# A decoder step in fp32: embedding first, S5 matrices on VectorE, products in column groups, last units by halves

## The chip, the cores and the metric

The kernel runs on one core of a Trainium2 chip. The metric is the device time of one execution in microseconds (us); a comparison uses the median over runs. The engines are named as in the profile: PE is TensorE (matmuls; PEld its weight loads), DVE is VectorE, ACT is ScalarE, POOL is GpSimd, and SP is SyncE, which here only issues DMAs.

## The reference

One inference step of a two-layer recurrent trunk, in fp32, for 512 prompt tokens and 8x8 sample tokens that share the weights. `h` is the stream of 1024 features by 576 tokens:

```python
for i in range(DEPTH):
    hn = rmsnorm(h, norm_mix[i])
    out = ab_mixer(hn) if i % 2 == 0 else cd_mixer(hn)
    h = h + out
    hn = rmsnorm(h, norm_ff[i])
    h = h + square(relu(hn @ w_ff1[i])) @ w_ff2[i]
    gate = sigmoid(rmsnorm(h, norm_ple[i]) @ w_ple_gate[i])
    h = h + gate * (p[i] @ w_ple_proj[i])
y = rmsnorm(h, norm_final)
```

`ab_mixer` holds an mLSTM and a retention (four heads each), `cd_mixer` an HGRN2 and an S5 state-space model with 32 groups of 16 channels and 64 complex states each. `rmsnorm(x, g)` is x / sqrt(mean(x^2) + 1e-6) * g over the 1024 features. The new states are outputs as well.

## The kernel before

The stream `h` lies in eight tiles of 128 features x 576 tokens. Every large product runs as three fp32r matmuls: an operand is split into a rounded high part and the rest, and hi*hi, hi*lo and lo*hi are added. A **unit** (`unit`, L222 to L232) is one 128x1024 block of weights: a DMA on SP's queue brings `wr`, ACT casts it to `wh` (L229), DVE subtracts to `wl` (L230), and `cols` runs 48 matmuls of 128x288 tokens (`mm3`, L238: 8 slices of the contraction, 3 products, 2 halves of the tokens). Inputs are split the same way: `xh` on ACT (L273) and `xl` on DVE (L274), for the MLP's middle `uh` (L270) and `ul` (L271).

`norm` makes the split inputs and the sum of squares `sqa`; its `stat` reduces the sum over partitions by a matmul with ones (L331), takes Ln and Exp(-0.5 x) on ACT and one Newton step on DVE, L279 to L281. `load` brings the embedding `pin` of layer 0, the first weights and `h`, multiplies the embedding (`po`, L361) and stores the eight results to DRAM from POOL's queue (L362); `po` has three buffers. `embed_in` loads and splits `pin`.

The S5 model turns into ordinary products with matrices that are made on the chip during the first MLP. `s5_tables` and `s5_turn` compute complex powers with many small DVE operations (128x32 and larger). `elem(ct)`, L1093 to L1109, builds a quarter of two matrices, ET and G: two multiplications and a sum for each, 128x1024 and 128x1152, with operands that are broadcast. `prod(ct, q)`, L1111 to L1137, transposes four groups of ET (L1120) and multiplies each with G into the rows 0 to 15 of a PSUM bank (L1121); ACT copies both out, and DMAs write them to DRAM. These pieces are hooks between the units of `ff` (layer 0): `elem` before a block, `prod` at its sixth and eighth unit.

`ple(1)` runs the last eight units. Six are ordinary: z = product * r (L481), tanh (L482), two DVE operations into `h` (L483, L484). `finish` does the last two by halves of the tokens, 288 each: for both halves the units, squares and the final statistic (L398, L399), Ln, Exp and Newton, and behind both the eight scalings of each half (L412) with a store each on SP's queue (L413).

The Tile framework orders the instructions: it places them by priority (`high_priority`, `issue_after`) and keeps each engine's stream in one order. An engine that waits holds back everything behind it in its stream.

Of the kernel before, what the change touches and what calls it, by code (L numbers as in the profile page):

```python
# [9 lines left out]
F32 = mybir.dt.float32  # L10
# [160 lines left out]
class K:  # L171
# [61 lines left out]
    def mm3(self, ps, wh, wl, xh, xl, first, last, halves=(0, 1)):  # L233

        mm = self.nc.tensor.matmul
        for a, b in ((wh, xh), (wh, xl), (wl, xh)):
            for j in halves:
                mm(ps[:, j, :HALF], a, b[:, j * HALF:(j + 1) * HALF],  # L238
                   start=first and a is wh and b is xh, stop=last and a is wl)
# [42 lines left out]

    def rsqrt(self, r, m, t):
# [9 lines left out]
    def norm(self, g, first=None, dve=False, tables=True):  # L293
# [17 lines left out]
        def stat():  # L311
            if not done:
                done.append(1)
                with self.tc.high_priority(400):
                    make()
            return r

        def make():

            tt = nc.vector.tensor_tensor  # L320
            hi, lo = (self.np_.tile([P, NT], F32R, name=f"sq{i}", tag="sq") for i in "hl")
            tt(acc[0], acc[0], acc[1], ALU.add)
# [10 lines left out]
            m, q = acc  # L333
            for j in range(2):
                s = slice(j * HALF, (j + 1) * HALF)
                nc.scalar.activation(r[:, s], ps[j], AF.Ln, bias=self.eps, scale=1.0 / D)
                nc.vector.tensor_scalar(m[:, s], ps[j], 1.0 / D, EPS, ALU.mult, ALU.add)
            nc.scalar.activation(r, r, AF.Exp, scale=-0.5)
            self.stat_done = self.newton(r, m, q)
# [26 lines left out]
    def embed_in(self, l, pool, eng, xp=None):  # L366
        self.xple = []
        for k in range(2):
            t = pool.tile([P, NT], F32, name="pin", tag="fu")
            eng.dma_start(t, self.A["pT"][l, k])  # L370
            self.xple.append(self.split(t, pool=xp or pool))

    def finish(self, n0, gate, pt):
# [14 lines left out]
        ws, rs = [gate(n) for n in range(n0, KD)], []  # L388
        for j in range(2):
            s = slice(j * HALF, (j + 1) * HALF)  # L390
            pst = self.pmt()[:, :HALF]
            for n, one in zip(range(n0, KD), ws):
                last = one(j)
# [7 lines left out]
            m, q, r = (pt.tile([P, HALF], F32, name=f"f{i}", tag=f"f{i}") for i in range(3))  # L401
            with self.tc.issue_after(last.ins):
                nc.scalar.preload_act_table_set("natural_log_exp_and_others")
            nc.scalar.activation(r, pst, AF.Ln, bias=self.eps, scale=1.0 / D)
            nc.vector.tensor_scalar(m, pst, 1.0 / D, EPS, ALU.mult, ALU.add)
            nc.scalar.activation(r, r, AF.Exp, scale=-0.5)
            self.newton(r, m, q)
            rs.append(r)
        for j in range(2):
            s = slice(j * HALF, (j + 1) * HALF)  # L410
# [1146 lines left out]
```

## Time and profile before

| | |
|---|---|
| median of 3 runs | 1700.53 us (1698.25 to 1702.41) |
| the profiled execution | 1699.72 us |
| its span in the trace | 1697.9 us |
| busy: PE / DVE / ACT / POOL | 1622.4 / 1004.9 / 604.4 / 308.0 us |
| granted PE clock, mean | 0.984 |
| moved by DMA | 168.92 MB |
| chain that ended last | PE 82%, DVE 10%, ACT 3%, DMA 3% |

The span is the time from the first to the last event of the profiled execution; 1.8 us lie around it. Times inside the trace count from the span's start. A row of a timeline gives start, duration, engine, line, operation, out<-in, shapes, count, and in brackets the idle time ahead of it and who ended it. Consecutive matmuls overlap in the pipeline, so the distance of two starts, not the duration, is the cost of one. The granted clock is the share of 2.4 GHz.

### The profile page before, as it was taken

How to read it: one execution, taken by the hardware profiler on the slowest of the kernel's cores; microseconds unless marked ns; L12 is line 12 of the kernel's file. 1: busy time of each engine (PE TensorE's matmuls, PEld its weight loads, DVE VectorE, ACT ScalarE, POOL GpSimd, SP SyncE). 2: the span in 40 equal slices, each digit the busy share in tenths (PEclk: the TensorE clock that was granted, in tenths of full speed). 3: DMA queues.
4: the chain of work that ended last, by engine and by line, in shares of the span. 5: the costliest groups of instructions: out<-in, count | busy, mean ns of one | idle time of the engine just before them, and what ended most of it. 6: DMA issues, size and time to landing. Idle time of an engine off the chain costs nothing.

```text
span 1697.9 us, 28934 instructions
## 1 busy us (share of the span) xinstructions
PE 1622.4 (96%) x11973; PEld 1564.9 (92%) x11973; DVE 1004.9 (59%) x1796; ACT 604.4 (36%) x952; POOL 308.0 (18%) x256
## 2 busy tenths in 40 slices
PE   6999999999899999999999789989999999999996
PEld 5999799999799999999999788979999999999996
DVE  5878665668943634447576797386643333334456
ACT  5333222235213223133443344362531323314354
POOL 1321232211300302003022565232100000000100
PEclk9999999999899999999999899999999999999998
DMA  6322222223222323324427322522222222222222
GB/s 247 108 80 89 99 82 89 78 78 114 92 92 93 123 87 95 114 87 142 143 71 222 119 72 68 151 84 64 75 86 77 88 87 78 85 88 92 85 87 69
DMA packets 77219, 168.92 MB, mean 99 GB/s; under 512 B 29088, under 2 KB 34080, under 8 KB 76960
## 3 DMA queue, kind: packets, MB, share of 16 engines
q1 hardware_dynamic: 76008, 164.20, 29.8%
q8 instruction: 94, 1.54, 0.4%
q0 software_dynamic: 640, 2.36, 0.3%
q10 hardware_dynamic: 440, 0.52, 0.1%
q14 instruction: 37, 0.30, 0.1%
HBM read 142.91 MB, written 24.13 MB: 98 GB/s over the span
## 4 chain that ended last, share of the span: by engine, by line
PE 82%; DVE 10%; ACT 3%; DMA 3%; issue 2%; SPq 0%; POOL 0%; ACTq 0%; DVEq 0%; POOLq 0%
PE pb L238 73%; PE pm L737 1%; PE pm L507 1%; DVE wl L230 1%; DVE e L1356 1%; DVE e L1358 1%; PE pm L1367 1%; PE pm L757 1%; PE pm L1121 1%; DMA s5U<-yd 1%; ACT xh L273 1%; PE pm L774 0%; DMA prd<-po 0%; DVE s5w L1204 0%; PE pm L849 0%
## 5 line engine op out<-in xcount | busy, mean ns | idle before, releaser
L238 PE MATMUL pb<-xh,wh 128*128 128x288 f32 x2480 | 544.0, 300 | 31.0 <-ACT wh L229 12.4
L238 PE MATMUL pb<-xl,wh 128*128 128x288 f32 x2480 | 542.7, 298 | 1.0 <-DVE xl L274 1.0
L238 PE MATMUL pb<-xh,wl 128*128 128x288 f32 x2480 | 543.1, 298 | 0.0
L229 ACT CAST wh<-wr 128x1024 fp32r<-128x1024 f32 x219 | 229.7, 1049 | 757.4 <-PE pb L238 701.5
L238 PEld LDWEIGHTS pb<-xh,wh 128*128 128x128 f32 x2480 | 402.7, 190 | 41.7 <-ACT wh L229 14.7
L238 PEld LDWEIGHTS pb<-xl,wh 128*128 128x128 f32 x2480 | 403.8, 190 | 6.1 <-issue 4.2
L238 PEld LDWEIGHTS pb<-xh,wl 128*128 128x128 f32 x2480 | 403.2, 190 | 3.6 <-issue 2.9
L230 DVE TENSOR_TENSOR wl<-wr,wh 128x1024 fp32r<-128x1024 f32 x199 | 251.0, 1261 | 22.8 <-ACT wh L229 13.5
L238 PE MATMUL pb<-ul,wh 128*128 128x288 f32 x1024 | 220.0, 296 | 6.6 <-DVE ul L271 6.6
L238 PE MATMUL pb<-uh,wl 128*128 128x288 f32 x1024 | 219.9, 296 | 1.5 <-DVE wl L230 1.5
L238 PE MATMUL pb<-uh,wh 128*128 128x288 f32 x1024 | 219.6, 296 | 0.2 <-ACT uh L270 0.2
L441 DVE TENSOR_TENSOR h<-h,pb 128x576 f32<-128x576 f32 x64 | 48.2, 753 | 214.0 <-PE pb L238 214.0
L238 PEld LDWEIGHTS pb<-ul,wh 128*128 128x128 f32 x1024 | 165.1, 189 | 6.8 <-DVE ul L271 6.8
L238 PEld LDWEIGHTS pb<-uh,wl 128*128 128x128 f32 x1024 | 165.0, 189 | 1.7 <-DVE wl L230 1.7
L238 PEld LDWEIGHTS pb<-uh,wh 128*128 128x128 f32 x1024 | 164.7, 189 | 0.8 <-issue 0.4
L428 DVE SCALAR_TENSOR_TENSOR fu<-pb,r 128x576 f32<-128x576 f32 x64 | 48.5, 757 | 185.5 <-PE pb L238 185.5
L308 POOL TENSOR_TENSOR sqa<-sqa,sq 128x576 f32<-128x576 f32 x20 | 32.8, 1640 | 502.1 <-ACT sq L307 481.3
L230 POOL TENSOR_TENSOR wl<-wr,wh 128x1024 fp32r<-128x1024 f32 x20 | 50.6, 2534 | 82.2 <-ACT wh L229 77.4
L271 DVE TENSOR_TENSOR ul<-fu,uh 128x576 fp32r<-128x576 f32 x64 | 52.3, 819 | 9.6 <-ACT uh L270 9.2
L1105 POOL TENSOR_TENSOR s5ET<-s5bc,s5y 128x1024 f32<-128x1024 f32 x4 | 8.3, 2066 | 260.7 <-PE pm L1121 221.2
L735 POOL TENSOR_TENSOR Vm<-V,cc 64x384 f32<-64x384 f32 (+3 forms) x36 | 34.6, 972 | 106.0 <-ACT V L719 66.8
L429 ACT ACTIVATE fu<-fu 128x576 f32<-128x576 f32 x64 | 43.8, 685 | 10.6 <-DVE fu L428 10.0
(456 smaller groups left out, 1631.7 us busy)
## 6 DMA issues: line engine op xcount, KB each, us to landing
wr<-in_w_dram SPq DMA_DIRECT2D x219, 512.0 KB, 3.5
sR<-Rd SPq DMA_DIRECT2D x12, 256.0 KB, 3.6
h<-in_hT_dram SPq DMA_DIRECT2D x8, 288.0 KB, 6.8
prd<-po POOLq DMA_DIRECT2D x8, 288.0 KB, 4.5
Gd<-s5G SPq DMA_DIRECT2D x4, 576.0 KB, 2.9
prj<-prd SPq DMA_DIRECT2D x8, 288.0 KB, 5.2
sG<-Gd SPq DMA_DIRECT2D x8, 288.0 KB, 6.6
out_yT_dram<-h SPq DMA_DIRECT2D x16, 144.0 KB, 1.9
```

Source lines behind the costliest of these rows:

```text
L229: nc.scalar.copy(hi, raw)
L230: (nc.gpsimd if self.lo_pool else nc.vector).tensor_tensor(lo, raw, hi.bitcast(F32), ALU.subtract)
L238: mm(ps[:, j, :HALF], a, b[:, j * HALF:(j + 1) * HALF], start=first and a is wh and b is xh, stop=last and a is wl)
L271: nc.vector.tensor_tensor(lo, src, hi.bitcast(F32), ALU.subtract)
L273: nc.scalar.mul(hi, src, scale)
L308: (nc.vector if i or dve else nc.gpsimd).tensor_tensor(acc[i], acc[i], t, ALU.add)
L428: nc.vector.scalar_tensor_tensor(self.sv(u), self.pv(ps), 0.0, self.sv(r()), ALU.max, ALU.mult)
L429: nc.scalar.activation(u, u, AF.Square)
L441: nc.vector.tensor_tensor(self.sv(self.h[n]), self.sv(self.h[n]), self.pv(ps), ALU.add)
L507: nc.tensor.transpose(dst, src[:n, t0:t0 + tn], self.ident[:n, :n])
L735: nc.gpsimd.tensor_tensor(Vm, V[:NS, 4, :n].unsqueeze(1).to_broadcast([NS, b1 - b0, n]), self.vmask[:, b0:b1].unsqueeze(2).to_broadcast([N ...
L737: nc.tensor.matmul(ps, Kt[:NS, 4], Vm.rearrange("p b n -> p (b n)"), start=True, stop=True)
```

## The change

- `unit` is divided into `fetch` (the DMA) and `parts` (cast and subtraction). `load` asks for the first weights, then the embedding, then the stream; DVE copies one column of the embedding into the first tile of `h`, so that this tile's DMA has to wait for the embedding. The splits of the embedding come behind both of its DMAs.
- `norm` adds epsilon in the sum of squares and runs Newton on the PSUM sum (`newton_sum`) by halves; two operations per norm (L337) go. The first mixer's statistic loses its raised priority.
- `elem` runs on DVE instead of POOL. `prod` does four transposes and then four products, each into its own 32 output rows; ACT copies the four results one by one.
- The last layer runs four ordinary units and the last four by halves of the tokens: half 0 of units 4 to 7, then half 1. Two units share a PSUM bank; the four weights stay in a pool of their own. The scalings and stores of a half stand right behind its statistic; in half 1 every other store goes to ACT's queue.

```diff
+    def fetch(self, *key):
         i = self.units.add(*key)
         raw = self.wp.tile([P, 8 * P], F32, name=f"wr{i}", tag="wr")
+        self.nc.sync.dma_start(raw, self.A["w"][i])
+        return raw
...
+    def newton_sum(self, r, ps, t):
+        nc = self.nc
+        nc.vector.tensor_tensor(t, r, r, ALU.mult)
+        nc.vector.scalar_tensor_tensor(t, t, -0.5 / D, ps, ALU.mult, ALU.mult)
         return nc.vector.scalar_tensor_tensor(r, t, 1.5, r, ALU.add, ALU.mult)
...
-            tt(acc[0], acc[0], acc[1], ALU.add)
+            stt(acc[0], acc[0], EPS * D / P, acc[1], ALU.add, ALU.add)
...
-                nc.vector.tensor_scalar(m[:, s], ps[j], 1.0 / D, EPS, ALU.mult, ALU.add)
...
             with self.tc.high_priority(60):
-                self.embed_in(0, lp, nc.sync)
-                ws = [self.unit("col2", "w_ple_proj", 0, 0, 0)]
+                raw = self.fetch("col2", "w_ple_proj", 0, 0, 0)
+                pin = self.embed_in(0, lp, nc.sync)
+                ws = [self.parts(raw)]
+                nc.vector.tensor_copy(self.h[0][:, 0:1], pin[1][:, 0:1])
             for k in range(KD):
                 nc.sync.dma_start(self.h[k], self.A["hT"][k])
...
-            tt = nc.gpsimd.tensor_tensor
+            tt = nc.vector.tensor_tensor
...
                 nc.tensor.transpose(pe[:, i * P:(i + 1) * P], ET[:, g].rearrange("p d h -> p (d h)"), self.ident)
-                nc.tensor.matmul(pk[:16, i * P:(i + 1) * P], ET[:, g, 0],
+            for i in range(4):
+                g = 4 * q + i
+                nc.tensor.matmul(pk[32 * i:32 * i + 16, :P], ET[:, g, 0],
                                  G[:, g, 0:8].rearrange("p d h -> p (d h)"), start=True, stop=True)
             f = lambda a: a.rearrange("p g n -> p (g n)")
             nc.scalar.copy(f(E), pe)
-            nc.scalar.copy(f(KT), pk[:16])
+            for i in range(4):
+                nc.scalar.copy(KT[:, i], pk[32 * i:32 * i + 16, :P])
...
-            for n in range(8 if l == 0 else 6):
+            for n in range(8 if l == 0 else 4):
...
+            with self.tc.tile_pool(name="wf", bufs=4) as wf:
+                ws = [self.unit("col", "w_ple_gate", l, n * P, 0, pool=wf) for n in range(4, 8)]
+                banks = {}
+                def gate(n, j):
...
+                self.finish(4, gate, pt)
```

In `finish` the loop over the halves now reads (its first part is as before):

```python
        for j in range(2):
...
            for n in range(n0, KD):
                last = gate(n, j)
...
            self.newton_sum(r, pst, q)
            for k in range(KD):
                stt(self.h[k][:, s], self.h[k][:, s], self.v("final", k), r, ALU.mult, ALU.mult)
                (nc.scalar if j and k % 2 else nc.sync).dma_start(self.A["yT"][k][:, s], self.h[k][:, s])
```

What the scheduler made of it, at three places. First DVE before, where `elem(0)` runs on POOL (L925 to L930 and L1018 to L1023 are the complex powers, L428 `fu`, L230 `wl` of unit 51):

```order
L1008 TENSOR_SCALAR s5y_4979<-s5yi 64x256
L927 TENSOR_TENSOR s5yr<-s5yr,s5p_w 128x32
L928 TENSOR_TENSOR s5yi<-s5p_5051,s5p_5052 128x32
L929 TENSOR_TENSOR s5p_w<-s5p_5052,s5p_5051 128x32
L1018 TENSOR_TENSOR s5p_5049<-s5yr 128x32
L930 TENSOR_TENSOR s5yi<-s5yi,s5p_w 128x32
L1019 TENSOR_TENSOR s5p_5050<-s5yi 128x32
L428 SCALAR_TENSOR_TENSOR fu<-pb,r 128x576
L1020 TENSOR_TENSOR s5p_5049<-s5p_5049,s5p_5050 128x32
L230 TENSOR_TENSOR wl_4991<-wr_4988,wh_4990 128x1024
```

and DVE with the change at the same place (L1126 to L1128 are `elem(0)`, L445 `fu`, L234 `wl` of units 51 and 52, L278 `ul`):

```order
L1126 TENSOR_TENSOR s5ET<-s5bc,s5y_4981 128x1024
L949 TENSOR_TENSOR s5yi<-s5p_5054,s5p_5055 128x32
L1127 TENSOR_TENSOR s5t<-s5bc,s5y_4982 128x8x128
L950 TENSOR_TENSOR s5p_w<-s5p_5055,s5p_5054 128x32
L1039 TENSOR_TENSOR s5p_5052<-s5yr 128x32
L445 SCALAR_TENSOR_TENSOR fu<-pb,r 128x576
L234 TENSOR_TENSOR wl<-wr_4991,wh 128x1024
L1128 TENSOR_TENSOR s5ET<-s5ET,s5t 128x1024
L951 TENSOR_TENSOR s5yi<-s5yi,s5p_w 128x32
L1126 TENSOR_TENSOR s5G<-s5bc,s5w_4975 128x1152
L278 TENSOR_TENSOR ul<-fu,uh 128x576
L1127 TENSOR_TENSOR s5t<-s5bc,s5w_4976 128x1152
```

The six operations of `elem(0)` now stand among the splits of the MLP. Second, PE at the third set of products, before:

```order
L238 MATMUL pb<-xh,wl_6904 128x288 x2
L1120 MATMUL pm<-cc,s5ET 128x128
L1121 MATMUL pm<-s5G,s5ET 16x128
L1120 MATMUL pm<-cc,s5ET 128x128
L1121 MATMUL pm<-s5G,s5ET 16x128
L1120 MATMUL pm<-cc,s5ET 128x128
```

and with the change (L1141 the transposes, L1144 the products, L245 bulk matmuls):

```order
L245 MATMUL pb<-ul,wh 128x288 x2
L1141 MATMUL pm<-cc,s5ET 128x128 x4
L1144 MATMUL pm<-s5G,s5ET 16x128
L245 MATMUL pb<-uh,wl 128x288 x2
L245 MATMUL pb<-uh,wh 128x288 x2
L245 MATMUL pb<-ul,wh 128x288 x2
```

The transposes stand together; of the products one follows them, and the other three come 524 bulk matmuls later. Third, DVE in the tail, before (L469 and L471, L472 are a half unit's z and its way into `h`; L405 and L279 to L281 the statistic of half 0; L412 its scalings):

```order
L405 TENSOR_SCALAR f_17197<-pm 128x288
L469 TENSOR_TENSOR z<-pb,r 128x288
L279 TENSOR_TENSOR f_17198<-f_17199 128x288
L280 SCALAR_TENSOR_TENSOR f_17198<-f_17198,f_17197 128x288
L471 SCALAR_TENSOR_TENSOR z<-z,prj_16661 128x288
L281 SCALAR_TENSOR_TENSOR f_17199<-f_17198,f_17199 128x288
L472 TENSOR_TENSOR h_128<-h_128,z 128x288
L412 SCALAR_TENSOR_TENSOR h_121<-h_121,vec,f_17199 128x288
```

and with the change (L429 the last scalings of half 0, L418 sums of squares of half 1, L501 to L504 unit 7's half 1, L293 the Newton step of half 1):

```order
L429 SCALAR_TENSOR_TENSOR h_127<-h_127,vec,f_17183 128x288
L429 SCALAR_TENSOR_TENSOR h_128<-h_128,vec,f_17183 128x288
L418 TENSOR_TENSOR sqa<-sqa,sq 128x288
L501 TENSOR_TENSOR z<-pb,r 128x288
L418 TENSOR_TENSOR sqa<-sqa,sq 128x288
L503 SCALAR_TENSOR_TENSOR z<-z,prj_16691 128x288
L504 TENSOR_TENSOR h_128<-h_128,z 128x288
L293 TENSOR_TENSOR f_17338<-f_17339 128x288
```

Before, the last half unit's z stands ahead of half 0's scalings; with the change it stands behind all eight of them.

## Rows read from the trace of the kernel before

**Rows 1.** The page: busy us (share) x instructions of each engine.

```profile
PE 1622.4 (96%) x11973; PEld 1564.9 (92%) x11973; DVE 1004.9 (59%) x1796; ACT 604.4 (36%) x952; POOL 308.0 (18%) x256
```

**Rows 2.** Timeline of PE at one set of products.

```profile
537.04 0.43 PE L238 MATMUL pb<-xh,wl 128*128 128x288 f32 x2
537.31 0.27 PE L1120 MATMUL pm<-cc,s5ET 128*128 128x128 f32 x1
...
539.26 0.39 PE L1121 MATMUL pm<-s5G,s5ET 128*16 128x128 f32 x2
539.58 0.53 PE L238 MATMUL pb<-xh,wh 128*128 128x288 f32 x2
```

**Rows 3.** Timeline of PE, 442 to 467 us, units 51 and 52.

```profile
442.81 0.43 PE L238 MATMUL pb<-uh,wh 128*128 128x288 f32 x2
...
457.87 0.85 PE L238 MATMUL pb<-ul,wh 128*128 128x288 f32 x2 [6.60 <-DVE ul L271]
...
462.83 0.53 PE L238 MATMUL pb<-uh,wh 128*128 128x288 f32 x2
...
466.92 0.43 PE L238 MATMUL pb<-uh,wh 128*128 128x288 f32 x2
```

**Rows 4.** Windows of PE: us, busy (x), granted clock, DMA share, GB/s.

```profile
458.00:460.00 2.00, 2.00 (x9) 0.50 0.61 241
```

**Rows 5.** Timeline of POOL at elem(0).

```profile
436.08 2.13 POOL L1105 TENSOR_TENSOR s5ET<-s5bc,s5y 128x1024 f32<-128x1024 f32 x1 [39.47 <-DVE s5y L1007]
```

**Rows 6.** Timeline of DVE, 436 to 455 us.

```profile
436.24 2.02 DVE L927 TENSOR_TENSOR s5yr<-s5yr,s5p_w 128x32 f32<-128x32 f32 x1
...
443.69 1.22 DVE L230 TENSOR_TENSOR wl<-wr,wh 128x1024 fp32r<-128x1024 f32 x1
...
446.24 0.19 DVE L927 TENSOR_TENSOR s5yr<-s5yr,s5p_w 128x32 f32<-128x32 f32 x1
...
451.14 3.26 DVE L230 TENSOR_TENSOR wl<-wr,wh 128x1024 fp32r<-128x1024 f32 x1
```

**Rows 7.** Groups of DVE by form: busy us, mean ns, idle before.

```profile
L770 DVE TENSOR_TENSOR hs<-hs,st 128x512 f32<-128x512 f32 x12 | 8.3, 691 | 0.3
```

**Rows 8.** Timeline of PE at two places of the first mixer.

```profile
72.60 0.71 PE L507 MATMUL pm<-cc,oT 128*128 128x128 f32 x5
73.06 0.38 PE L238 MATMUL pb<-xl,wh 128*128 128x288 f32 x1
...
89.36 1.08 PE L757 MATMUL pm<-s_in,qd 128*32 128x129 f32 x16
90.37 0.40 PE L238 MATMUL pb<-xl,wh 128*128 128x288 f32 x1
90.61 0.43 PE L238 MATMUL pb<-xh,wl 128*128 128x288 f32 x2
```

**Rows 9.** Groups of DVE by form, the norms.

```profile
L337 DVE TENSOR_SCALAR sqa<-pm 128x288 f32<-128x288 f32 x12 | 5.2, 458 | 8.3 <-ACT r L336 8.3
```

**Rows 10.** Tile h, first 40 us: ns (least/median/most), first and last start.

```profile
L352 SPq DMA_DIRECT2D h<-in_hT_dram x8: 328/432/705, 2.1 to 8.9; - x8
```

**Rows 11.** DMA issues of the first 45 us: KB each, median us to landing.

```profile
h<-in_hT_dram SPq DMA_DIRECT2D x8, 288.0 KB, 6.8
```

**Rows 12.** Timeline of ACT, the fourth and the seventh po.

```profile
23.99 1.73 ACT L361 ACTIVATE po<-pb 128x576 f32<-128x576 f32 x3
...
30.36 1.36 ACT L361 ACTIVATE po<-pb 128x576 f32<-128x576 f32 x2 [1.46 <-DMA prd<-po]
```

**Rows 13.** Timeline of PE in the start.

```profile
31.77 0.53 PE L331 MATMUL pm<-sqh,ones 128*128 128x288 f32 x2 [3.70 <-ACT po L361]
```

**Rows 14.** Timeline of PE, its last two rows.

```profile
1681.23 0.65 PE L398 MATMUL pm<-sqa,ones 128*128 128x288 f32 x2
1686.23 1.33 PE L399 MATMUL pm<-sq,ones 128*128 128x288 f32 x2 [4.35 <-ACT sq L395]
```

**Rows 15.** Timeline of DVE, the scalings of the last half.

```profile
1690.88 3.52 DVE L412 SCALAR_TENSOR_TENSOR h<-h,vec,f 128x288 f32<-128x288 f32 x8
```

**Rows 16.** Timeline of ACT in the tail, a table load.

```profile
1675.03 1.28 ACT L403 ACT_TABLE_LOAD   x1
```

More of the change, by code (lines that the diff above doesn't have):

```diff
@@ L231, in unit, with mm3 @@
         return hi.rearrange("p (k n) -> p k n", k=8), lo.rearrange("p (k n) -> p k n", k=8)
-    def mm3(self, ps, wh, wl, xh, xl, first, last, halves=(0, 1)):
+    def unit(self, *key, pool=None):
+        return self.parts(self.fetch(*key), pool)
+    def mm3(self, ps, wh, wl, xh, xl, first, last, halves=(0, 1), bank=None):
         mm = self.nc.tensor.matmul
@@ L313, in stat @@
                 done.append(1)
-                with self.tc.high_priority(400):
+                if tables:
+                    with self.tc.high_priority(400):
+                        make()
+                else:
                     make()
@@ L366, in embed_in @@
     def embed_in(self, l, pool, eng, xp=None):
-        self.xple = []
+        self.xple, ts = [], []
         for k in range(2):
@@ L387, in finish @@
                 (nc.vector if k > 3 else nc.gpsimd).tensor_tensor(acc, acc, t, ALU.add)
-        ws, rs = [gate(n) for n in range(n0, KD)], []
+        nc.vector.tensor_scalar(acc, acc, EPS * D / P, None, ALU.add)
         for j in range(2):
@@ L459, in ple @@
             xs, r = self.norm(f"ple{l}", xq)
-            def gate(n):
-                w = self.unit("col", "w_ple_gate", l, n * P, 0)
-                ps = self.bulk()
-                def half(j):
-                    s = slice(j * HALF, (j + 1) * HALF)
-                    for k in range(8):
-                        self.mm3(ps, w[0][:, k], w[1][:, k], xs[k][0], xs[k][1], k == 0, k == 7, (j,))
-                    z = pt.tile([P, NT], F32, name="z", tag="z")[:, :HALF]
-                    nc.vector.tensor_tensor(z, ps[:, j, :HALF], r()[:, s], ALU.mult)
-                    last = nc.scalar.activation(z, z, AF.Tanh, scale=0.5)
-                    nc.vector.scalar_tensor_tensor(z, z, 1.0, prj[n][:, s], ALU.add, ALU.mult)
-                    nc.vector.tensor_tensor(self.h[n][:, s], self.h[n][:, s], z, ALU.add)
-                    return last
-                return half
-            for n in range(8 if l == 0 else 6):
+            for n in range(8 if l == 0 else 4):
                 w = self.unit("col", "w_ple_gate", l, n * P, 0)
@@ L484, in ple @@
                 nc.vector.tensor_tensor(self.h[n], self.h[n], z, ALU.add)
-            if l == 1:
-                self.finish(6, gate, pt)
+            if l == 0:
+                return
+            with self.tc.tile_pool(name="wf", bufs=4) as wf:
+                ws = [self.unit("col", "w_ple_gate", l, n * P, 0, pool=wf) for n in range(4, 8)]
+                banks = {}
+                def gate(n, j):
+                    s = slice(j * HALF, (j + 1) * HALF)
+                    w = ws[n - 4]
+                    if n % 2 == 0:
+                        banks[j] = self.bulk()
+                    ps = banks[j]
+                    for k in range(8):
+                        self.mm3(ps, w[0][:, k], w[1][:, k], xs[k][0], xs[k][1], k == 0, k == 7, (j,), n % 2)
+                    z = pt.tile([P, NT], F32, name="z", tag="z")[:, :HALF]
+                    nc.vector.tensor_tensor(z, ps[:, n % 2, :HALF], r()[:, s], ALU.mult)
+                    last = nc.scalar.activation(z, z, AF.Tanh, scale=0.5)
+                    nc.vector.scalar_tensor_tensor(z, z, 1.0, prj[n][:, s], ALU.add, ALU.mult)
+                    nc.vector.tensor_tensor(self.h[n][:, s], self.h[n][:, s], z, ALU.add)
+                    return last
+                self.finish(4, gate, pt)
     def out_proj(self, name, k0, xs):
```

40 lines of the change are left out of this document (17 added, 23 removed).

## Prediction

> **What bounds the kernel now.** I read the page's table of engines first, then the list of what TensorE waited for, then TensorE's timeline around the largest waits, and last the timelines of the engines named there. TensorE is busy 96% of the span [rows 1]: the kernel is a stream of 128x288 matmuls, two of which take 0.27 us (537.04 to 537.31) [rows 2], so 0.133 us each and about 6.3 us for a unit of 48. Only three things can shorten it: less work on TensorE, fewer stalls of it, or a shorter tail behind its last matmul. The change touches one large stall, 64 small matmul passes, the start and the tail.
>
> **The stall by the S5 tables.** From 442.81 to 466.92 TensorE does 96 matmuls [rows 3], the two units 51 and 52. At 0.133 us that is 12.8 us; it took 24.1. So 11.3 us were lost: 6.60 us in one wait for a `ul` of DVE [rows 3], some 2 us in shorter ones, and the rest in the matmuls behind it, which ran at the granted clock of 0.50, the 1.2 GHz level [rows 4], until 462.83. The cause stands in two timelines. POOL starts `elem(0)` at 436.08 with an operation of 2.13 us [rows 5], and DVE's 128x32 operation at 436.24 takes 2.02 us, where the same operation takes 0.19 us at 446.24; under POOL's second group a `wl` subtraction takes 3.26 us instead of 1.22 [rows 6]. DVE is held for as long as POOL's large operations run, and `wl`, `fu` and `ul` queue behind it.
>
> The change puts these six operations on DVE itself. Price: none of them runs there now. A two-operand one of the same size costs 1.22 us [rows 6], and one with a broadcast operand 0.691 us for 512 elements [rows 7], 1.35 ns an element. I take 1.22 us for 1024 elements and 1.36 for 1152, in all 7.7 us, because rows 7 show a broadcast at the plain rate. The bound above is POOL's 2.13 us [rows 5].
>
> Now I lay DVE's new order on the old clock. The tables end at 436.3; two multiplications to 438.9; `fu` to 439.8; `wl` of unit 51 to 441.0 (needed four matmuls into the unit, 443.3); the sum for ET to 442.2; the first for G to about 443.7, if its small input, asked for at 438.9, is in within 3.5 us; `ul` to 444.4 (needed 447.7); then `fu`, `wl` of unit 52 to 447.7 (needed 449.5), the last sum to 449.0 and `ul` to 449.8. TensorE's order is new too: it asks for that `ul` only after 70 matmuls and four transposes, at about 452. Nothing is late, by a margin of about 2 us; the whole 11.3 us go. At POOL's 2.13 us per operation `wl` of unit 52 comes near 452 and 2.5 to 3 us are lost again. So **-11.3 us**, between -8.5 and -11.3. The groups for the other three quarters of the tables cost TensorE nothing before and their `ul` has 3 us of margin in the new order: nothing.
>
> The page "Vector Engine (DVE) Microarchitecture Reference" of the Trainium skill (Measured stream behaviour on trn2) speaks against this: a port streams at full rate only over runs of at least two adjacent words, else near 1.7 times as long, and the tables are read with each word repeated 16 times. By that the four multiplications would take about 2.1 us each and the term would be about -9.6; rows 7, whose operand repeats one word 128 times, speak against it, and I give it 0.15, within the forecast.
>
> **The products.** A set is four transposes and four products of 16 columns, alternating, from 537.31 to 539.58 [rows 2]: 2.27 us, and the next bulk pair starts 0.1 us late. There are eight sets. A product is two passes of 0.16 us (539.26 to 539.58, [rows 2]). The trace has both new forms already. Transposes back to back: five in 0.46 us, 0.092 each [rows 8]. Small matmuls into changing groups of 32 output partitions: sixteen passes in 1.01 us, 0.063 each, and 0.11 us on the next bulk matmul [rows 8]. A set becomes 0.37 + 8 x 0.063 + two changes of 0.1 = 1.1 us, a gain of 1.3; eight make 10.2. The new order splits the sets (in four of them one product runs alone or far from the other three), which adds some seven changes of 0.1 to 0.2 us. So **-9.0 us**. Bounds: no overlap, 0.16 a pass, leaves the gain of the transposes less the changes, about -2; above, -10.2. The four copies that replace one on ACT lie in ACT's idle time beside the bulk matmuls.
>
> "TensorEngine Tiling (Array Packing)" (Key Properties) of the Trainium skill says that a change of tiling mode drains TensorE, though tiles of one mode work in parallel. Its cost is in the 0.11 us behind the sixteen passes of rows 8, if those run tiled; if not, each of some 15 switches costs more, and the second rival holds.
>
> **The norms.** Two operations of 0.458 us per norm go, twelve in all [rows 9]; they lie beside matmuls except where TensorE waits for the new h. I take **-0.5 us**, with the reshuffled order in the first mixer's heads as an unknown of -2 to +4.
>
> **The start.** The stream h is not asked for later: only its first piece waits for the embedding, so it is now asked for last, and seven of eight keep their place in the queue. Its landing is that of the old last piece, issued at 8.9 plus 6.8 us [rows 10, 11], about 15.6. ACT now begins with the embedding, so the first matmuls come some 2 us sooner, but ACT then stands until 15.6 and has eight casts, squares and a `wh` before the fourth `po`, which I put at 24.6 instead of 23.99 [rows 12]. The seventh `po` waits for a buffer: its predecessor's store is done 6.4 us after the fourth began (30.36 - 23.99, [rows 12]). That makes 31.0; and on ACT the cast of the squares and another `wh` now stand before the eighth, so TensorE goes on near 33.9 instead of 31.77 [rows 13]. Against that, small stalls behind 59 us may go. **+1.5 us**, between -2 and +4.
>
> **The tail.** TensorE's last bulk matmul ends at about 1681.2 as before [rows 14]; the sum of matmuls is the same. In the new order the first half of unit 7 is done 72 matmuls and a statistic earlier, 1671.3. From there: z and tanh to 1672.5; two table loads of 1.28 us [rows 16], because the logarithm's table is asked for and the next tanh takes it back, 1675.1; tanh, square, DVE's two operations and the next square, 1677.0; load, logarithm, load, exponential, 1680.5. Then DVE in its own order: seven half-width operations of 0.46 us, 1683.8; the eight scalings of half 0, 3.52 us [rows 15], 1687.3; and only behind them z of unit 7's second half, whose matmuls ended at 1681. Behind it in a line: z, tanh, table load, square to 1690.4, statistic of 1.33 us [rows 14] to 1691.8, logarithm and exponential to 1692.9, three Newton operations to 1694.3, eight scalings to 1697.9. Before, the last scaling ended at 1694.4 [rows 15]. So the halves do not shorten the tail, they lengthen it: **+3.4 us**, between +1 and +4.5; half 0's stores leave early, which helps nobody.
>
> **Sum.** 1699.7 (the profiled execution) - 11.3 - 9.0 - 0.5 + 1.5 + 3.4 = 1683.8. The median of the runs is 0.8 above the profiled one: **1684.6 us**.
>
> **Rivals.**
> A, DVE becomes the bound (slower). If a broadcast operation costs s us on DVE, each table group delays the `ul` behind five of them by 5(s - 1.29), less 2 us of margin at the first and 3 at the other three. The forecast's gain of 16 is eaten at s = 2.65, above POOL's 2.13; at 3.0 the loss is 23 and the time 1700.5 + 7 = 1707. For it: POOL's rows. Against: rows 6 and 7. Chance 0.06.
> B, the column groups do not overlap and switches cost: products at -2, 1691.6. For it: the rows of the products now, 0.16 a pass. Against: rows 8. Chance 0.14.
> C, the tail gains: if half 0's exponential comes 3 us sooner (one load less), the scalings end before z of the second half is due and the tail is 3 us shorter than forecast or more: 1680. Against: the order of ACT. Chance 0.08.
> D, the start does not do what it says and costs more: the late first piece holds the norm, and all matmuls behind it, 4 us longer than I put: 1689. Chance 0.08.
> The forecast has 0.64.
>
> **Numbers.** The runs agree within about 0.3%, 5 us, which is what a measurement can tell from no change. The range takes the forecast's unknowns and rivals B, C and D: 1675 to 1696. Faster by over 0.3% (below 1695.4) is everything but A and the worst of B and D together: 0.89; same 0.07; slower 0.04.
>
> **What would show it.** No wait of TensorE between 440 and 460 and no low clock there; DVE's six operations at 1.2 to 1.4 us; sets of products near 1.1 us; TensorE's restart near 34 us; the last scaling 16 to 17 us behind the last bulk matmul, before 13. It is wrong if the products stay at 0.16 us a pass, if a broadcast operation takes 2 us, or if z of the last half precedes the scalings.

## The result and the profile after

The changed kernel takes 1682.93 us (median of 4 runs, 1680.36 to 1686.05); the kernel before, run beside it, 1700.62 us (4 runs). The ratio is 0.9892, 95% interval 0.9878 to 0.9906: 1.1% faster. The forecast was 1684.6 us, its range 1675 to 1696. The profiled execution took 1683.24 us, its span is 1681.4 us, 16.5 us shorter than before. Of all runs told of below one, an execution of `e4a_scale_later`, took 8853.81 us; it is in no ratio, and its cause is not known. The page's engine line, against [rows 1]:

```profile
PE 1614.6 (96%) x11973; PEld 1561.7 (93%) x11973; DVE 1007.2 (60%) x1834; ACT 606.5 (36%) x980; POOL 248.3 (15%) x232
```

TensorE has the same 11973 instructions and is busy 7.8 us less, though its bulk matmuls are the same: what went are mostly the slow small matmuls and the low clock in the stall, less the low clock that the new start brought. POOL lost 60 us to DVE, yet DVE's busy time grew by 2 only: its own operations no longer stretch under POOL's, and the norms are shorter.

**Where the time went.** ACT casts one `wh` per unit, 219 in all, so the start of a cast, counted from 0, shows how far each kernel is. Before and after, in us, from ACT's timeline:

| cast of unit | before | after | gained so far | what lies since the line above |
|---|---|---|---|---|
| 24 | 223.69 | 223.84 | -0.15 | start, first norm, first mixer |
| 48 | 417.78 | 417.92 | -0.14 | first half of the MLP |
| 72 | 586.75 | 574.20 | 12.55 | `elem(0)`, one pair of product sets |
| 88 | 693.84 | 679.03 | 14.81 | one pair of sets |
| 104 | 800.98 | 783.89 | 17.09 | one pair of sets |
| 112 | 858.05 | 837.62 | 20.43 | one pair of sets, `elem(3)` |
| 140 | 1161.71 | 1142.78 | 18.93 | second mixer |
| 212 | 1630.03 | 1611.11 | 18.92 | rest of the last layer |
| end | 1697.9 | 1681.4 | 16.5 | the tail |

The two middle pairs of sets gained 2.3 us each. The first and the last stretch with products are not such plain pairs: of its 32 transposes the changed kernel does 12 in the first and only 4 in the last. By the starts of TensorE's matmuls, the small ones and the late bulk matmuls behind them took 4.75 us a pair before; in the four stretches they now take 3.38, 2.47, 2.46 and 1.51. So the products gained 1.37 + 2.28 + 2.29 + 3.24 = 9.2 us, and of the 12.69 us between casts 48 and 72 the stall gave 11.3 (12.69 - 1.37).

**The tables.** DVE's timeline from 435 us, where [rows 6] had operations of 2 and 3 us:

```profile
436.06 1.21 DVE L1126 TENSOR_TENSOR s5ET<-s5bc,s5y 128x1024 f32<-128x1024 f32 x1
437.20 0.17 DVE L949 TENSOR_TENSOR s5yi<-s5p,s5p 128x32 f32<-128x32 f32 x1
437.30 1.21 DVE L1127 TENSOR_TENSOR s5t<-s5bc,s5y 128x1024 f32<-128x1024 f32 x1
...
439.31 1.21 DVE L234 TENSOR_TENSOR wl<-wr,wh 128x1024 fp32r<-128x1024 f32 x1
440.44 1.21 DVE L1128 TENSOR_TENSOR s5ET<-s5ET,s5t 128x1024 f32<-128x1024 f32 x1
...
441.68 1.34 DVE L1126 TENSOR_TENSOR s5G<-s5bc,s5w 128x1152 f32<-128x1152 f32 x1
442.95 0.74 DVE L278 TENSOR_TENSOR ul<-fu,uh 128x576 fp32r<-128x576 f32 x1
...
448.16 0.74 DVE L278 TENSOR_TENSOR ul<-fu,uh 128x576 fp32r<-128x576 f32 x1
```

A multiplication with a repeated operand takes as long as the `wl` beside it, 1.21 us, and the 128x32 operations take 0.17. The first `ul` is done at 443.7, the second at 448.9. TensorE's windows in this stretch, against [rows 4]:

```profile
458.00:460.00 2.00, 2.00 (x17) 1.00 0.01 2
440.00:470.00 30.00, 30.00 (x229) 1.00 0.43 145
```

It is busy for all 30 us at a clock of 1.00, the 2.4 GHz level. Neither the wait of 6.60 us nor the low clock of [rows 3, 4] is left.

**The products.** TensorE's timeline at two places where [rows 2] had four alternating pairs:

```profile
540.53 0.43 PE L245 MATMUL pb<-xh,wl 128*128 128x288 f32 x2
540.89 0.41 PE L1144 MATMUL pm<-s5G,s5ET 128*16 128x128 f32 x8
541.23 0.53 PE L245 MATMUL pb<-xh,wh 128*128 128x288 f32 x2
...
803.64 0.60 PE L1141 MATMUL pm<-cc,s5ET 128*128 128x128 f32 x4
804.17 0.41 PE L1144 MATMUL pm<-s5G,s5ET 128*16 128x128 f32 x8
```

Eight passes take 0.34 us (540.89 to 541.23), 0.042 each. The gained time grows by 2.26 and 2.28 us over the two middle pairs of sets, so a set costs 1.13 us less.

**The tail.** DVE's timeline, last 17 us:

```profile
1664.32 3.52 DVE L429 SCALAR_TENSOR_TENSOR h<-h,vec,f 128x288 f32<-128x288 f32 x8
1667.75 0.45 DVE L418 TENSOR_TENSOR sqa<-sqa,sq 128x288 f32<-128x288 f32 x1
1668.12 0.45 DVE L501 TENSOR_TENSOR z<-pb,r 128x288 f32<-128x288 f32 x1
...
1673.13 0.46 DVE L293 TENSOR_TENSOR f<-f 128x288 f32<-128x288 f32 x1 [3.11 <-ACT f L426]
...
1674.61 3.52 DVE L429 SCALAR_TENSOR_TENSOR h<-h,vec,f 128x288 f32<-128x288 f32 x8
```

ACT's, half 0's exponential:

```profile
1661.26 0.45 ACT L426 ACTIVATE f<-f 128x288 f32<-128x288 f32 x1
```

and TensorE's, against [rows 14]:

```profile
1660.42 0.41 PE L245 MATMUL pb<-xh,wh 128*128 128x288 f32 x1 [0.91 <-DVE z L501]
...
1663.61 0.29 PE L245 MATMUL pb<-xh,wl 128*128 128x288 f32 x1
1668.99 1.33 PE L419 MATMUL pm<-sqa,ones 128*128 128x288 f32 x2 [5.09 <-DVE sqa L418]
```

The last bulk matmul ends near 1663.74 (1663.61 + 0.133). Its result is read at 1668.12 only, behind eight scalings of the other half; the last scaling ends at 1678.13, 14.4 us behind the bulk matmuls, where it was 13.2 before ([rows 14, 15]: 1694.4 - 1681.23). The last bulk matmul comes later as well: it ends 52.6 us behind the start of cast 212 (1663.74 - 1611.11), before 51.2 (1681.23 - 1630.03), and 0.91 of these 1.4 us are the wait for z at 1660.42.

### The profile page after: what moved, and what is told of

Its sections match the earlier page's. It is cut to its first block, busy times and chain, and to the rows that moved or that the text cites. A ratio compares the mean times of both kernels' runs of the same rounds, so it can differ in the third digit from the quotient of the medians.

```text
span 1681.4 us, 28961 instructions
## 1 busy us (share of the span) xinstructions
PE 1614.6 (96%) x11973; PEld 1561.7 (93%) x11973; DVE 1007.2 (60%) x1834; ACT 606.5 (36%) x980; POOL 248.3 (15%) x232
## 4 chain that ended last, share of the span: by engine, by line
PE 82%; DVE 9%; ACT 3%; DMA 3%; issue 2%; SPq 1%; DVEq 0%; ACTq 0%
PE pb L245 75%; PE pm L758 1%; DVE e L1380 1%; PE pm L528 1%; PE pm L778 1%; DMA s5U<-yd 1%; DVE e L1382 1%; PE pm L870 0%; DVE xl L281 0%; PE pm L795 0%; SPq L1201 0%; ACT xh L280 0%; DVE s5w L1230 0%; ACT wh L233 0%; DVE h L429 0%
## 5 line engine op out<-in xcount | busy, mean ns | idle before, releaser
L245 PE MATMUL pb<-xh,wh 128*128 128x288 f32 x2480 | 547.3, 300 | 31.9 <-DVE z L1337 9.2
L245 PE MATMUL pb<-xl,wh 128*128 128x288 f32 x2480 | 547.3, 299 | 0.1
L245 PE MATMUL pb<-xh,wl 128*128 128x288 f32 x2480 | 545.4, 298 | 0.0
L245 PEld LDWEIGHTS pb<-xh,wh 128*128 128x128 f32 x2480 | 404.8, 191 | 40.7 <-issue 13.5
L245 PEld LDWEIGHTS pb<-xl,wh 128*128 128x128 f32 x2480 | 405.1, 190 | 6.8 <-issue 5.8
L245 PEld LDWEIGHTS pb<-xh,wl 128*128 128x128 f32 x2480 | 405.1, 190 | 4.0 <-issue 3.2
L234 DVE TENSOR_TENSOR wl<-wr,wh 128x1024 fp32r<-128x1024 f32 x199 | 245.0, 1231 | 24.0 <-ACT wh L233 15.4
L245 PE MATMUL pb<-uh,wl 128*128 128x288 f32 x1024 | 219.1, 295 | 0.0
L245 PE MATMUL pb<-ul,wh 128*128 128x288 f32 x1024 | 218.7, 295 | 0.0
L245 PE MATMUL pb<-uh,wh 128*128 128x288 f32 x1024 | 218.6, 295 | 0.0
L245 PEld LDWEIGHTS pb<-uh,wl 128*128 128x128 f32 x1024 | 163.9, 188 | 0.6 <-DVE s5R L951 0.4
L245 PEld LDWEIGHTS pb<-uh,wh 128*128 128x128 f32 x1024 | 163.8, 188 | 0.6 <-issue 0.6
L245 PEld LDWEIGHTS pb<-ul,wh 128*128 128x128 f32 x1024 | 164.1, 188 | 0.0
L445 DVE SCALAR_TENSOR_TENSOR fu<-pb,r 128x576 f32<-128x576 f32 x64 | 48.3, 756 | 180.1 <-PE pb L245 179.9
L234 POOL TENSOR_TENSOR wl<-wr,wh 128x1024 fp32r<-128x1024 f32 x20 | 50.4, 2521 | 90.6 <-ACT wh L233 90.6
L278 DVE TENSOR_TENSOR ul<-fu,uh 128x576 fp32r<-128x576 f32 x64 | 48.3, 756 | 9.5 <-ACT uh L277 9.4
L281 DVE SCALAR_TENSOR_TENSOR xl<-h,vec,xh 128x576 fp32r<-128x576 f32 x48 | 40.8, 862 | 11.7 <-ACT xh L280 11.7
```

The source lines that it names most:

```text
L234: (nc.gpsimd if self.lo_pool else nc.vector).tensor_tensor(lo, raw, hi.bitcast(F32), ALU.subtract)
L245: mm(ps[:, j if bank is None else bank, :HALF], a, b[:, j * HALF:(j + 1) * HALF], start=first and a is wh and b is xh, stop=last and a is wl)
L278: nc.vector.tensor_tensor(lo, src, hi.bitcast(F32), ALU.subtract)
L281: nc.vector.scalar_tensor_tensor(lo, src, scale, hi.bitcast(F32), ALU.mult, ALU.subtract)
L445: nc.vector.scalar_tensor_tensor(self.sv(u), self.pv(ps), 0.0, self.sv(r()), ALU.max, ALU.mult)
```

## The experiments

Each is the changed kernel with one edit (`e4b_one_load` and `e9_both` have two), beside runs of the kernel before on the same chip, whose median lies between 1700.31 and 1701.98 us; the changed kernel's own runs stand above. The four runs of a kernel lie 2 to 8 us apart (the one execution named above aside), so a difference of medians under about 2 us is read from the traces or left undecided. "Gain" is the column of the table above, for that kernel's profiled execution. Two stretches change from one profiled execution to the next without an edit in them: the start, by some 1.5 us (last section), and the second mixer (casts 112 to 140), whose gain runs from -4.7 us in `e7_all_wait` to +1.9 in `e9_both`. A trace's gain at its end is therefore not all the edit's.

### The tables back on POOL, and only the first quarter on DVE

`e1_pool`:

```diff
-            tt = nc.vector.tensor_tensor
+            tt = nc.gpsimd.tensor_tensor
```

> The changed kernel with elem back on POOL, all else kept. My theory (DVE is held while POOL's large operations run, and wl, fu and ul queue behind it): DVE operations of over 2 us between 435 and 460 come back, TensorE waits some 7 to 9 us there and runs at the low clock behind it; 9 to 12 us slower than the changed kernel, near 1693. Rival (the gain there came from the new places of the transposes and products, not from the engine): under 3 us slower, near 1685.

Measured 1693.32 us (ratio 0.9953, 0.9936 to 0.9969), 10.4 above the changed kernel. DVE's timeline:

```profile
437.26 2.03 DVE L948 TENSOR_TENSOR s5yr<-s5yr,s5p_w 128x32 f32<-128x32 f32 x1
439.21 2.08 DVE L949 TENSOR_TENSOR s5yi<-s5p,s5p 128x32 f32<-128x32 f32 x1
...
452.31 3.31 DVE L234 TENSOR_TENSOR wl<-wr,wh 128x1024 fp32r<-128x1024 f32 x1
```

and TensorE's wait that comes of it:

```profile
459.09 0.85 PE L245 MATMUL pb<-ul,wh 128*128 128x288 f32 x2 [6.45 <-DVE ul L278]
```

The windows of TensorE behind it:

```profile
459.00:463.00 4.00, 3.91 (x17) 0.54 0.37 145
463.00:467.00 4.00, 4.00 (x32) 1.00 0.39 133
```

The held operations, the wait and the low clock of [rows 3, 4] are back, with everything else of the change in place. By the starts of TensorE's matmuls from 445 to 463 us the stall costs 9.9 us here, near the 10.4 of the medians.

`e1b_first` puts `elem(0)` alone on DVE:

```diff
-            tt = nc.vector.tensor_tensor
+            tt = (nc.vector if ct == 0 else nc.gpsimd).tensor_tensor
```

> elem(0) on DVE, elem(1) to elem(3) on POOL. My theory (the other three groups cost TensorE nothing wherever they run): within 1 us of the changed kernel, near 1683, though DVE operations beside POOL's are stretched again. Rival (each group on POOL costs something): 3 us slower or more.

Measured 1681.34 us (0.9884, 0.9869 to 0.9899), not to be told from the changed kernel. The whole gain of this part is the first quarter's.

### The products, two by two

The change does two things to a set: transposes ahead of products, and four column groups. `e2_prod_old` undoes both, with one ACT copy of 16x512:

```diff
-            for i in range(4):
-                g = 4 * q + i
-                nc.tensor.matmul(pk[32 * i:32 * i + 16, :P], ET[:, g, 0],
+                nc.tensor.matmul(pk[:16, i * P:(i + 1) * P], ET[:, g, 0],
...
```

> The changed kernel with the products as before: each product follows its transpose, all in output rows 0 to 15, one copy of 16x512 in ACT. Theory: a set takes 2.27 us again, as in the kernel before, and every pair of sets gives back the 2.27 us that the changed kernel gained: 9 us slower than the changed kernel, 1692. Rival (most of the 9 us of those stretches came from the new place of the elementwise operations or of the ul, and not from TensorE's small matmuls): within 3 us of the changed kernel, 1683 to 1686.

`e3_one_group` keeps the order and gives up the groups:

```diff
-                nc.tensor.matmul(pk[32 * i:32 * i + 16, :P], ET[:, g, 0],
+                nc.tensor.matmul(pk[:16, i * P:(i + 1) * P], ET[:, g, 0],
...
```

> Transposes first as in the changed kernel, but the four products all into rows 0 to 15 as before, one copy on ACT. My theory (the passes overlap because they go into different groups of 32 output partitions): passes again 0.16 us apart, 0.78 us more for each of eight sets, 6.2 us slower, near 1689. Rival (the gain came from no longer alternating transposes and products): 0.1 us a pass or less, under 1.5 us slower, near 1684.

`e8_alt_groups` keeps the groups and gives up the order:

```diff
-            for i in range(4):
-                g = 4 * q + i
                 nc.tensor.matmul(pk[32 * i:32 * i + 16, :P], ET[:, g, 0],
```

> The changed kernel with the products in four column groups, but each again behind its own transpose: the fourth case of the two by two with the changed kernel, the one with one group, and the one with the old products. Theory (what the old form paid for is the alternation: each transpose behind a product costs 0.25 us, and two passes of one group cannot overlap with another group's): a set takes 1.9 to 2.3 us, a pair of sets gives back at least 1.6 of the 2.27 us, and the time is 1689 to 1692. Rival (the column groups alone make a pass cheap, 0.042 us, and with it the change): a set takes 1.4 us or less, the time 1683 to 1686.

| | rows 0 to 15 alone | four column groups |
|---|---|---|
| product behind each transpose | 1690.66 us, gain over units 88 to 104: 0.0 | 1689.79 us, gain 0.0 |
| four transposes, then products | 1685.01 us, gain 1.5 | 1682.93 us, gain 2.3 |

(Ratios: `e2_prod_old` 0.9944, 0.9926 to 0.9962; `e8_alt_groups` 0.9940, 0.9924 to 0.9956; `e3_one_group` 0.9912, 0.9895 to 0.9929. In the first set the scheduler put transposes and products together in all four kernels, so the order differs in the other seven.) TensorE's timeline of `e8_alt_groups`, half a set:

```profile
647.91 0.27 PE L1141 MATMUL pm<-cc,s5ET 128*128 128x128 f32 x1
648.11 0.39 PE L1142 MATMUL pm<-s5G,s5ET 128*16 128x128 f32 x2
648.43 0.33 PE L1141 MATMUL pm<-cc,s5ET 128*128 128x128 f32 x1
648.69 0.39 PE L1142 MATMUL pm<-s5G,s5ET 128*16 128x128 f32 x2
```

and of `e3_one_group`:

```profile
646.38 0.60 PE L1141 MATMUL pm<-cc,s5ET 128*128 128x128 f32 x4
646.91 1.05 PE L1144 MATMUL pm<-s5G,s5ET 128*16 128x128 f32 x8
647.89 0.53 PE L245 MATMUL pb<-xh,wh 128*128 128x288 f32 x2
```

In column groups but alternating, two passes take 0.32 us, to the hundredth what they took before [rows 2]: the groups are worth nothing there, where no product of another group stands beside them. Without groups but together, a pass takes 0.12 us (0.98 for eight), and with both 0.042. Four transposes take 0.53 us together (646.38 to 646.91) and about 0.25 each when they alternate. So a quarter of the old 0.16 a pass and half of the old 0.25 a transpose went into the change between the two, and the order brings about two thirds of the gain (1.5 of 2.3), the groups the rest once the order allows it. My 6.2 us for the loss of the groups alone was wrong: it is 2.1 by the medians and 0.7 per pair by the traces.

### The tail

`e3t_tail_old` is the tail of the kernel before: six ordinary units, two by halves, both statistics ahead of the scalings.

```diff
-            for n in range(8 if l == 0 else 4):
+            for n in range(8 if l == 0 else 6):
...
-                self.finish(4, gate, pt)
+                self.finish(6, gate, pt)
```

> The changed kernel with the tail of the kernel before: two last units by halves, both statistics before any scaling, stores from SP alone. Theory (the four units by halves lengthen the tail by 1 to 2.4 us, since half 0's scalings run ahead of the last half unit's z): last scaling 13 us behind the last bulk matmul, and 1.2 to 2.4 us faster than the changed kernel, 1680.5 to 1681.7. Rival (the new tail is worth something): slower than the changed kernel by 2 us or more.

Measured 1679.81 us (0.9881, 0.9861 to 0.9900), 3.1 below the changed kernel. TensorE's and DVE's timelines:

```profile
1660.14 0.65 PE L419 MATMUL pm<-sqa,ones 128*128 128x288 f32 x2
...
1669.80 3.52 DVE L433 SCALAR_TENSOR_TENSOR h<-h,vec,f 128x288 f32<-128x288 f32 x8
```

Its last scaling ends 13.2 us behind the bulk matmuls (1669.80 + 3.52 against 1660.14). From the start of cast 212 to the end of the span the old tail takes 67.9 us, here and in the kernel before; the new one takes 70.3 in all nine kernels that have it, alike to 0.02 us. So the new tail costs 2.4 us, and what the two medians differ by beyond that is not the tail's.

`e4a_scale_later` keeps the four units by halves and moves half 0's scalings behind the last half unit:

```diff
+            if j:
+                with self.tc.issue_after(add.ins):
+                    scale(0)
...
+        scale(1)
```

> The eight scalings of half 0 placed behind unit 7's half 1 on DVE, so that they run while ACT and TensorE do half 1's statistic. My theory (the scalings ahead of that z are what lengthens the tail): the last scaling ends 12 us behind the last bulk matmul instead of 14.4; 2.4 us faster, near 1680.5. Rival (the statistic's chain on ACT with its table loads sets the end whatever DVE does): within 0.5 us of the changed kernel, 1683.

Measured 1680.56 us (1680.45 without the one execution named above; 0.9876, 0.9859 to 0.9892). DVE's timeline:

```profile
1663.14 0.45 DVE L511 TENSOR_TENSOR z<-pb,r 128x288 f32<-128x288 f32 x1
...
1664.97 3.52 DVE L415 SCALAR_TENSOR_TENSOR h<-h,vec,f 128x288 f32<-128x288 f32 x8
...
1669.87 3.52 DVE L415 SCALAR_TENSOR_TENSOR h<-h,vec,f 128x288 f32<-128x288 f32 x8
```

The z comes first, the scalings fill the time until the other half's Newton step, and the last scaling ends 11.8 us behind the bulk matmuls (1673.39 - 1661.58): 2.6 less than in the changed kernel. So DVE's order cost 2.6 us of that tail. But the halves are no gain either: the bulk matmuls still end 1.4 us later than with the old tail (52.6 us behind cast 212), and from that cast to the end this tail takes 67.7 us, the old one 67.9.

`e4b_one_load` adds that the logarithm's table is asked for early in half 1 alone:

```diff
-            with self.tc.issue_after(last.ins):
-                nc.scalar.preload_act_table_set("natural_log_exp_and_others")
+            if j:
+                with self.tc.issue_after(last.ins):
+                    nc.scalar.preload_act_table_set("natural_log_exp_and_others")
```

> The changed kernel with half 0's scalings behind the last half unit on DVE, as in the run before, and the logarithm's table asked for early only for half 1. Theory (the early request for half 0 costs two table loads of 1.28 us in the middle of the tanh operations, which hold z and so TensorE's last matmuls by 0.9 us): one such pair of loads goes, TensorE's last wait for z goes, the time is 2.4 to 3.5 us below the changed kernel, 1679 to 1680.5. Rival (the loads lie beside matmuls): no different from the run without this edit, 1680.6, within 0.5.

Measured 1678.76 us (0.9880, 0.9855 to 0.9905; 1677.28 to 1685.28). ACT's timeline of the changed kernel, where the table asked for early is thrown out by the next tanh:

```profile
1653.67 1.28 ACT L424 ACT_TABLE_LOAD   x1
1654.96 1.28 ACT L502 ACT_TABLE_LOAD   x1
1656.25 0.45 ACT L502 ACTIVATE z<-z 128x288 f32<-128x288 f32 x1
```

Both loads are gone in `e4b_one_load`, but TensorE's wait of 0.9 us for z stays in all three kernels, so that reason of mine was wrong. The last scaling stands 11.5 us behind the bulk matmuls instead of 11.8, and the tail from cast 212 takes 67.4 us; the 1.8 us between the medians are not decided.

### The start and the norms

`e5_start_old`, the old order of the loads:

```diff
-                raw = self.fetch("col2", "w_ple_proj", 0, 0, 0)
-                pin = self.embed_in(0, lp, nc.sync)
-                ws = [self.parts(raw)]
-                nc.vector.tensor_copy(self.h[0][:, 0:1], pin[1][:, 0:1])
+                self.embed_in(0, lp, nc.sync)
+                ws = [self.unit("col2", "w_ple_proj", 0, 0, 0)]
...
```

> The changed kernel with the start of the kernel before: the embedding's casts stand ahead of the weights in the old order, no piece of the stream waits for it. Theory (the new start brings the first matmuls forward by about 3 us and the first mixer loses most of it again): unit 8 starts about 3 us later than in the changed kernel, unit 48 within 1.5 us of it; the time is 0 to 2 us above the changed kernel, 1683 to 1685. Rival (the late piece of the stream costs time at the end of the start): 1 to 3 us faster than the changed kernel, 1680 to 1682.

Measured 1684.34 us (0.9907, 0.9891 to 0.9924). By the medians the new start is worth 1.4 us, by the traces the old one 1.0 at unit 24 (gain 0.83 against -0.15): nothing that these runs can tell. The first cast is 2.3 us earlier with the new start, but at unit 8 the kernels differ by 0.4 only, not by the 3 that I expected. TensorE's timeline of the changed kernel

```profile
23.37 0.85 PE L245 MATMUL pb<-xh,wh 128*128 128x288 f32 x2 [5.07 <-ACT po L380]
...
30.79 0.53 PE L245 MATMUL pb<-xh,wh 128*128 128x288 f32 x2 [1.92 <-ACT po L380]
```

and of `e5_start_old`

```profile
31.21 0.53 PE L245 MATMUL pb<-xh,wh 128*128 128x288 f32 x2 [4.10 <-ACT po L377]
```

show why: both go on near 31 us, behind a `po`, and ACT's `po` waits for the store of an older one in both. ACT's timelines of the changed kernel and of `e5_start_old`:

```profile
28.02 0.66 ACT L380 ACTIVATE po<-pb 128x576 f32<-128x576 f32 x1 [2.48 <-DMA prd<-po]
...
29.80 1.36 ACT L377 ACTIVATE po<-pb 128x576 f32<-128x576 f32 x2 [1.86 <-DMA prd<-po]
```

Whatever begins earlier waits there. It also pays with the clock: behind the wait of 5.07 us TensorE is granted 0.51 from 24 to 28 us in the changed kernel, and 1.00 in `e5_start_old`, whose two waits between 20 and 24 us are 0.59 and 1.62 us:

```profile
24.00:28.00 4.00, 3.11 (x24) 1.00 0.85 286
```

`e6_norm_old`, the old norm with the raised priority of the first mixer's statistic:

```diff
-                if tables:
-                    with self.tc.high_priority(400):
-                        make()
-                else:
+                with self.tc.high_priority(400):
...
-            stt(acc[0], acc[0], EPS * D / P, acc[1], ALU.add, ALU.add)
+            tt(acc[0], acc[0], acc[1], ALU.add)
...
+                nc.vector.tensor_scalar(m[:, s], ps[j], 1.0 / D, EPS, ALU.mult, ALU.add)
...
```

> The changed kernel with the norm of the kernel before: two more DVE operations of 0.46 us a norm, and the first mixer's statistic with the old high priority. Theory (the shorter norm and the order that goes with it give the 1.3 us that the changed kernel gains between units 7 and 8, also where the start is the old one): that gain goes, unit 8 starts 1 to 2 us later, the time is 1 to 2 us above the changed kernel, 1684 to 1685. Rival (the norms lie beside matmuls, nothing): within 0.7 of the changed kernel, and the gain between units 7 and 8 stays.

Measured 1685.99 us (0.9913, 0.9895 to 0.9931). Between units 7 and 8 the changed kernel gains 1.4 us, as every kernel here with the new norm does, and this one loses 0.3; at unit 24 it is 2.0 us later than the changed kernel, at unit 212 3.4. So the norm's edits are worth some 2 us. That size is rough: `e8_alt_groups`, with the new norm, is at unit 24 only 0.2 us ahead of this kernel. Which of the two, shorter norm or dropped priority, was not tried.

`e7_all_wait` lets every piece of the stream wait for the embedding:

```diff
-                nc.vector.tensor_copy(self.h[0][:, 0:1], pin[1][:, 0:1])
+                for k in range(KD):
+                    nc.vector.tensor_copy(self.h[k][:, 0:1], pin[1][:, 0:1])
```

> The changed kernel with all eight pieces of the stream waiting for the embedding, not the first alone. Theory (the DMA engines are full until 24 us, so the pieces, now behind some 2 MB of other loads, land up to 5 us later, and the norm with its statistic follows): unit 4 starts 2 to 5 us later than in the changed kernel, the time is 1685 to 1688. Rival (the order of the loads does not matter while the DMA engines are full, since ACT has the embedding and its products to do meanwhile): unit 4 within 1 us, 1682 to 1684.

Measured 1680.44 us (0.9880, 0.9859 to 0.9901): my theory fell. The pieces are asked for at 7.8 to 12.7 us instead of 2.1 to 7.9, and unit 4 still starts 0.8 us earlier than in the changed kernel; the clock, told of in the last section, is better in this execution and worth some 1.5. Nor were the DMA engines full until 24 us: in the changed kernel's trace their share is about 1.0 from 4 to 20 us and 0.37 from 20 to 24. The order of these loads costs nothing that these runs can tell.

### Both together

`e9_both` has the tail of `e4b_one_load` and the start of `e7_all_wait`.

> The tail of the run with one early table load for half 1 and scalings behind the last half unit, and the start of the run in which all eight pieces of the stream wait for the embedding, in one kernel. Theory (the two lie 1600 us apart and add up: 2.9 us in the tail, and the 1.2 us wait for hs between units 22 and 24 that did not appear in the run with that start): last scaling 11.5 us behind the last bulk matmul, no wait for hs in the first mixer, 1676 to 1679. Rival (the start's gain is given back in the second mixer, whose waits change from kernel to kernel): 1679 to 1681, no different from either.

Measured 1676.15 us (1673.98 to 1678.88; 0.9855, 0.9834 to 0.9877): the fastest of all, 6.8 below the changed kernel by the medians. The last scaling ends 11.2 us behind the bulk matmuls (1665.38 + 3.52 against 1657.60 + 0.133), and TensorE's list of waits from 75 to 240 us has no wait for `hs` any more, nor has that of `e7_all_wait`; the changed kernel has one of 1.2 us. In its trace 3.4 us more come from the second mixer, which neither edit touches.

## Why the prediction was right, point by point

- **The S5 stall** (-11.3): from unit 48 to 72 the kernel gained 12.69 us; less 1.37 for the products in it, 11.3, the whole of it as forecast. Putting the tables back on POOL costs 10.4 by the medians and 9.9 in that stretch of the trace. The mechanism is shown: no wait and no low clock there, and both return with POOL. The order laid by hand held, the first `ul` done at 443.7 (444.4 predicted) and the second at 448.9 (449.8). The operations took 1.21 us for 1024 elements and 1.34 for 1152, near the 1.22 and 1.36 taken from [rows 6, 7]. "Vector Engine (DVE) Microarchitecture Reference" of the Trainium skill (Measured stream behaviour on trn2) gives full rate only to runs of at least two adjacent words. The prediction carried that over to words that are repeated 16 times, and for these the trace shows no such price. Rival A had its price at 2.65 us and is out.
- **The products** (-9.0): 9.2 by the starts of TensorE's matmuls. The size was right and the reason only in part. The step that failed is the lower bound, and rival B with it: "no overlap, 0.16 a pass". That 0.16 was not the price of a pass in one group, but of a pass beside a transpose; without overlap it is 0.12, and the loss 2 us rather than 7. "TensorEngine Tiling (Array Packing)" of the Trainium skill (Key Properties) says that different tiles can run in parallel and that a change of tiling mode drains TensorE. The trace agrees with the first: 0.042 us a pass in four groups, 0.12 in one. Of the second it shows only that changes between transpose and product cost: the same four transposes and eight passes in one group take 1.51 us together (646.38 to 647.89) and 2.27 alternating [rows 2]. That a drain is what they pay for is not shown, and in column groups the alternating set costs as much.
- **Norms and start** (-0.5 and +1.5): together a loss of 0.15 us at unit 24, where 1.0 was predicted. The sum was near, the parts were off, and they are not well separated: the norms gave some 2 us, and the start lost 1.0 by the trace of `e5_start_old` and gained 1.4 by its medians. TensorE went on at 30.79, not 33.9: the seventh `po` had its buffer at 28.02 instead of 31.0, and the eighth followed at 30.08. Rival D is out.
- **The tail** (+3.4): +2.4 by the table, and z of the last half behind all eight scalings, as laid out. Two steps were mis-sized. "TensorE's last bulk matmul ends at about 1681.2 as before" put at nothing what measured 1.4 us, the wait of 0.91 us for z among them. And half 0's exponential was put 0.7 us ahead of the last bulk matmul's end and came 2.0 ahead (1661.71 against 1663.74). The operations between it and the scalings took 2.6 us (1661.71 to 1664.32) instead of 3.3, so the eight scalings began 2.0 us earlier; hence 14.4 us behind the bulk matmuls instead of 16 to 17. Rival C needed a 3 us shorter tail. The experiments built that tail; the change did not.
- **What no term held**: the second mixer gave back 1.5 us. That is within what this stretch differs by from kernel to kernel (-4.7 to +1.9), and its cause was not looked for further.

The sum of the predicted terms is -15.9, the span's change -16.5. That they lie so near is in part luck: the norms and the start came 0.85 us and the tail 1.0 us cheaper than forecast, and the second mixer, which no term held, took 1.5 us back. Two signs that the prediction named did not come: TensorE's restart near 34 us was at 30.79, and the last scaling 16 to 17 us behind the last bulk matmul was at 14.4.

## What to carry to other kernels

An elementwise operation on POOL can cost more than its own time, because DVE's small operations stretch to its length (0.19 us to 2 us here); before moving work off the busier engine, look whether that engine's operations grow under it. Put small matmuls of one shape together before arranging them in column groups: here the second was worth nothing without the first. When work is cut into halves to shorten a tail, check on the engine both halves share that nothing of the first stands ahead of the last input of the second, and count what the halves cost TensorE: here 1.4 us, nearly all that the better order gained over the old tail.

## What the runs showed that was not expected

TensorE's clock in the start differed between executions whose code is the same up to there. After the wait near 31 us the changed kernel's windows of TensorE show

```profile
24.00:28.00 4.00, 4.00 (x18) 0.51 0.83 262
28.00:32.00 4.00, 2.08 (x14) 0.92 0.42 168
32.00:36.00 4.00, 4.00 (x23) 0.65 0.85 249
```

and those of `e1b_first`

```profile
24.00:28.00 4.00, 4.00 (x19) 0.50 0.82 253
28.00:32.00 4.00, 2.36 (x16) 0.95 0.44 177
32.00:36.00 4.00, 4.00 (x32) 1.00 0.83 254
```

In both it had waited 5.1 us for a `po` and run near the 1.2 GHz level from 24 to 28. Behind the second wait, 1.92 us in the one and 1.64 in the other, it fell back to that level in the changed kernel for most of four microseconds and not at all in `e1b_first`. Among the profiled executions of kernels with the new norm and an early first matmul, six have 1.00 from 32 to 36 us and start unit 4 between 2.3 and 3.1 us ahead of the kernel before; five have 0.58 to 0.66 and start it 0.8 to 1.5 ahead. So some 1.5 us between such kernels go with this clock and with no edit; what decides it was not tried.
